# Sample-state updates cut from 128 rows to row blocks of 32, and both halves' C products added into one PSUM bank

## The chip, the cores and the metric

The kernel runs on one NeuronCore of a Trainium2 chip. The metric is device time in microseconds for one execution. The core has five engines with instruction queues of their own: TensorE (PE, matmuls and weight loads), VectorE (DVE), ScalarE (ACT), GpSimd (POOL) and SyncE (SP, which issues DMAs here). TensorE's results go to PSUM banks of 128 x 512 floats, from which VectorE and ScalarE take them.

## What is computed

One step of a hybrid decoder layer for two groups of tokens: a prompt of 272 tokens (16 meta tokens and 256) and 8 sample sequences of 4 tokens each, 304 tokens in all, 1024 channels. A SwiGLU feed-forward, a mixer, another SwiGLU, a last norm. The mixer's branch B is a state-space scan with 32 heads of 64 channels in 4 groups; B and C (128 state entries) are shared by the 8 heads of a group. The part that the change touches is the scan of the sample sequences, which bring a state of their own:

```
decay = jnp.exp(acs[:, :, -1:] - acs)
states = jnp.einsum('bcsgn,bcsgr,bcsgrp->bcgrpn', bc, decay, xdt)
chunk_decay = jnp.exp(acs[:, :, -1])
def step(h, inp):
    s, d = inp
    return h * d[..., None, None] + s, h
y_off = jnp.einsum('bcqgn,bcgrpn,bcqgr->bcqgrp', cc, h_prev, jnp.exp(acs))
```

For a sample sequence there is one chunk of 4 tokens: its new state is the old one times a decay, plus a sum over the 4 tokens of B times the decayed input; its outputs get C times the old state.

## The kernel before

**The work and its order.** `program()` writes out the order of some 1960 weight tiles of 128 x 128: first feed-forward, gates, projections into the mixer (`x`, then `ac`, `ah`, `ab`, `ya`, `z`, `gb`, `yb`, `wo`), second feed-forward. Each tile gives three one-pass matmuls (L255 to L257: high weights by high inputs, high by low, low by high), with 288 to 304 columns. I call them projections below. A unit of 8 tiles is loaded by SyncE (L174, four buffers), split into a high part by ScalarE (L183, `whi`) and a low part by VectorE (L184, `wlo`).

**The scan beside it.** The scan runs as two generators, `prompt()` and `sample()` (L904, L1039), that `drive` advances a step at a time between projections. The framework's scheduler then reorders the instructions of each engine by its own estimate, so the order of the built program isn't that of the source. Each queue runs in order. Four PSUM banks (`pss`, tag "s") are for the scan, four (`psm`, tag "m") for the projections' sums.

**The sample scan.** There are 4 groups g, and the 8 sequences come in two halves q of 4: eight units u = 2g + q. A unit's old state is a tile of 128 state entries x 4 sequences x 512 channels (`ht`, three buffers, 1 MB, loaded at L1051 and stored at L1104). For each unit:

- C by old state (L1131): four products, one for each sequence j, into partitions 32j of one bank. They are matmuls of full precision, two instructions each, 32 columns of the array by 512. ScalarE copies the bank (L1133, `yr`), four transposes turn it (L1138), VectorE multiplies by the decay (L1141).
- For each sequence, VectorE multiplies the state by its decay (L1150), TensorE makes the sum over tokens (L1152, one pass, 128 rows x 128 columns, 512 moving columns), VectorE adds it from PSUM (L1153).

The 128 rows of L1152 are the 32 sample tokens in four copies: `four` (L894) replicates the tokens, and rows 32 to 63 and 96 to 127 of the B side, and 64 to 127 of the input side, hold what rounding left over (L865, L1064), so that one pass carries all four products of high and low parts. Which sequence is meant is picked by a mask: ScalarE makes four masked copies of B for a unit (L1125, `bm`), in which 16 of the 128 rows are not zero.

`tokens(g)` (L1067) makes the inputs of a group: four transposes of the replicated sample tokens (L1078), products with dt and decay on VectorE, and the same for the prompt's last 16 tokens, whose side (`xl`, `bl`) the prompt scan uses in a matmul of 128 rows (L985), added to L984's sum. `diagonal` (L1091) makes the part within the 4 tokens, with matmuls of 48 rows and 64 columns (L1095).

`setup` (L726) runs once, some 100 us earlier: dt, its running sums by 32 small matmul instructions (L781 to L807), masks, and B's replicated side (L854 to L866).

Of the kernel before, what the change touches and what calls it, by code (L numbers as in the profile page):

```python
# [9 lines left out]
F32 = mybir.dt.float32  # L10
F32R = mybir.dt.float32r
# [6 lines left out]
P = 128  # L18
# [103 lines left out]
def tile_step(ctx: ExitStack, tc: tile.TileContext, wst: bass.AP, xT: bass.AP, vec: bass.AP,  # L122
# [469 lines left out]
    ssd = Scan(tc, mp, pss, dram, xs, V, K, h0, o_hp, o_hs)  # L592
# [113 lines left out]
class Scan:  # L706
# [3 lines left out]
    def __init__(self, tc, mp, pss, dram, xs, V, K, h0, o_hp, o_hs):  # L710
        self.nc, self.sp, self.pss, self.dram = tc.nc, mp, pss, dram
# [14 lines left out]
    def setup(self, psd, xp):  # L726
# [9 lines left out]
        act.activation(reps[:, 0].rearrange("p (k t) -> p k t", t=NL),  # L736
                       raw[:, TL:S0].unsqueeze(1).to_broadcast([P, P // NL, NL]), AF.Copy)
        act.activation(reps[:, 1].rearrange("p (k t) -> p k t", t=NB * NT),
                       raw[:, S0:T].unsqueeze(1).to_broadcast([P, 4, NB * NT]), AF.Copy)

        gtl = xp.tile([NL, P // NL, NL], F32, name="gtl")
        act.activation(gtl, K[0:NL, C_GT:C_GT + NL].unsqueeze(1).to_broadcast([NL, P // NL, NL]), AF.Copy)
# [37 lines left out]
        dl = da[0:NL, 2]  # L780
        te.matmul(pv[:, 0], lhsT=K[:, C_GT:C_GT + P], rhs=da[:, 0], start=True, stop=True)  # L781
        te.matmul(pv[:, 1], lhsT=K[:, C_GT:C_GT + P], rhs=da[:, 1], start=True, stop=False)
        te.matmul(pv[:, 1], lhsT=K[0:NL, C_ONE:C_ONE + P], rhs=dl, start=False, stop=True)
        te.matmul(pv[:, 2], lhsT=gtl.rearrange("p k t -> p (k t)"), rhs=dl, start=True, stop=True)
        te.matmul(pv[:, 3], lhsT=K[0:32, C_GTS:C_GTS + P], rhs=da[0:32, 3], start=True, stop=True)
        te.matmul(pv[:, 4], lhsT=K[:, C_ONE:C_ONE + P], rhs=da[:, 1], start=True, stop=False)
        te.matmul(pv[:, 4], lhsT=K[0:NL, C_ONE:C_ONE + P], rhs=dl, start=False, stop=True)
# [3 lines left out]
        NS = NB * NT  # L791
        NX = NS + NL


        p = self.ps()
        tri = K[:, C_TRI:C_TRI + P]
        self.cum = self.t("cum", [P, 3, H])
        te.matmul(p[:, 0:2 * H].rearrange("p (i c) -> p i c", c=H), lhsT=tri, rhs=da[:, 0:2], start=True, stop=True)
        te.matmul(p[0:32, 2 * H:3 * H], lhsT=K[0:32, C_TRIS:C_TRIS + 32], rhs=da[0:32, 3], start=True, stop=True)
        te.matmul(p[32:64, 2 * H:3 * H], lhsT=K[0:NL, C_TRI:C_TRI + 32], rhs=dl, start=True, stop=True)  # L800
        q = p[0:32, P:]
        for i in range(2):
            te.matmul(q[:, P * i:P * (i + 1)], lhsT=da[:, i], rhs=tri, start=True, stop=True)
        te.matmul(q[:, TL:S0], lhsT=da[:, 1], rhs=K[:, C_ONE:C_ONE + NL], start=True, stop=False)
        te.matmul(q[:, TL:S0], lhsT=dl, rhs=K[0:NL, C_TRI:C_TRI + NL], start=False, stop=True)
        te.matmul(q[:, S0:T], lhsT=da[0:32, 3], rhs=K[0:32, C_TRIS:C_TRIS + 32], start=True, stop=True)
        te.matmul(q[:, T:T + NL], lhsT=dl, rhs=K[0:NL, C_TRI:C_TRI + NL], start=True, stop=True)  # L807
# [22 lines left out]
        act.activation(self.mk[:, 0:P - NM], tri[:, NM:P], AF.Copy)  # L830
        act.activation(self.mk[:, P - NM:2 * P - NM], tri, AF.Copy)
        act.activation(self.mk[:, 2 * P - NM:], K[:, C_ONE:C_ONE + NL], AF.Copy)
        mks = xp.tile([NX, NX], F32, name="mks")
        pool.memset(mks, 0.0)
        act.activation(mks[0:NS, 0:NS], K[0:NS, C_TRIS:C_TRIS + NS], AF.Copy)
        act.activation(mks[NS:NX, NS:NX], K[NS:NX, C_TRI + NS:C_TRI + NX], AF.Copy)
# [17 lines left out]
        for what in ("bs", "bl"):  # L854
            rep = self.four(xp, XC, what == "bl")
            yield
            p = self.ps()
            for g in range(G):
                te.transpose(p[:, g * P:(g + 1) * P], rep[:, g], ident)
            bs = self.t(what, [P, G, P], dt=F32R)  # L860
            setattr(self, what, bs)
            pv = p.rearrange("p (g n) -> p g n", g=G)
            act.activation(bs, pv, AF.Copy)
            for a in (32, 96):
                dve.tensor_tensor(out=bs[a:a + 32], in0=pv[a:a + 32], in1=bs[a:a + 32].bitcast(F32), op=ALU.subtract)  # L865
            yield  # L866
# [5 lines left out]
    def exps(self):  # L872
# [11 lines left out]

        even = self.t("even", [P, 1])
        act.activation(even, K[:, C_BM:C_BM + 1], AF.Copy)
        for b in range(1, NL // NT):
            dve.tensor_tensor(out=even, in0=even, in1=K[:, C_BM + b:C_BM + b + 1], op=ALU.add)
        dve.tensor_scalar(out=self.dtr[:, 2], in0=self.dtr[:, 2], scalar1=even, scalar2=None, op0=ALU.mult)
# [4 lines left out]
    def four(self, pl, c0, tail=False):  # L894

        a, n = (TL, NL) if tail else (S0, NB * NT)
        self.n += 1
        r = pl.tile([P, 4, P // n, n], F32, name=f"four{self.n}", tag="tmp", bufs=2)
        src = self.xs[:, c0:c0 + 4, a:a + n].unsqueeze(2).to_broadcast([P, 4, P // n, n])
        for j in range(4):  # L900
            self.nc.scalar.activation(r[:, j], src[:, j], AF.Copy)
        return r.rearrange("p j k t -> p j (k t)")
# [136 lines left out]
    def sample(self):  # L1039
# [27 lines left out]
        def tokens(g):  # L1067
# [3 lines left out]
            for o, i in ((xst, 3), (self.xl, 2)):  # L1071
                if i == 2:
                    rep[g] = self.four(self.sp, 4 * g, True)
                    yield
# [166 lines left out]
```

## Time and profile before

| what | value |
|---|---|
| median of three runs | 881.22 us (879.95 to 882.02) |
| the profiled execution | 881.86 us |
| its span from first to last instruction | 880.0 us |
| TensorE busy | 868.8 us, 6448 matmuls |
| VectorE busy | 621.3 us |
| ScalarE busy | 496.2 us |
| mean granted TensorE clock | 0.996 |
| sample updates L1152 | 32 matmuls, 378 to 559 us into the span |
| products with C, L1131 | 64 instructions |

How to read it: a group of the profile is a line of the code with an engine, an operation, what is written and read (`out<-in`), the shape, and the number of instructions; then busy time and the mean duration in ns. PEld is TensorE's weight load, which can overlap a matmul. A shape such as 128\*32 at a matmul is the rows and columns of the array in use. A timeline row starts with the start and the duration in us. Neighbouring matmuls overlap in the records, so a matmul's price is read from the distance between starts.

### The profile page before, as it was taken

The numbers are of one execution on the slowest core, as the hardware profiler recorded it, in microseconds if no ns is written. First come the engines' busy times: TensorE is split into PE (matmuls) and PEld (weight loads), VectorE is DVE, ScalarE is ACT, GpSimd is POOL, SyncE is SP. The second block draws the span as 40 slices with busy tenths as digits, with TensorE's granted clock in tenths as the row PEclk, the third lists the DMA queues.
The fourth block names the chain that finished last, engine by engine and source line by source line (L and its number), as shares of the span: only waits on it lengthen the run. The fifth ranks groups of instructions, "written<-read, shape, count | busy, mean of one in ns | idle before, by whom it ended". The sixth has DMA issues, their size and how long they took to land.

```text
span 880.0 us, 16239 instructions
## 1 busy us (share of the span) xinstructions
PE 868.8 (99%) x6448; PEld 849.8 (97%) x6448; DVE 621.3 (71%) x996; ACT 496.2 (56%) x899; POOL 53.4 (6%) x86
## 2 busy tenths in 40 slices
PE   9999999999999999999999999999999999999996
PEld 7999999999999999999999899999999999999996
DVE  6756666554677798799988999886676666665443
ACT  8543434343667787966655687774465444444442
POOL 0000000000012233001000211100000000000000
PEclk9999999999999999999999999999999999999999
DMA  8554545454644545865666655755555555555541
GB/s 299 190 155 157 165 147 167 146 166 150 201 166 146 153 153 171 314 211 202 231 223 225 242 198 174 257 183 169 167 168 166 164 165 166 163 164 168 169 139 54
DMA packets 45851, 158.69 MB, mean 180 GB/s; under 512 B 7168, under 2 KB 9504, under 8 KB 43472
## 3 DMA queue, kind: packets, MB, share of 16 engines
q1 hardware_dynamic: 45344, 157.21, 54.6%
q8 instruction: 50, 0.82, 0.4%
q10 hardware_dynamic: 432, 0.46, 0.2%
q14 instruction: 25, 0.20, 0.1%
HBM read 145.34 MB, written 12.31 MB: 179 GB/s over the span
## 4 chain that ended last, share of the span: by engine, by line
PE 97%; DVE 1%; ACT 1%; DMA 1%; SPq 0%; issue 0%; DVEq 0%
PE ps_d L257 6%; PE ps_d L256 5%; PE ps_d L255 5%; PE ps_u L257 5%; PE ps_g L255 5%; PE ps_u L256 5%; PE ps_u L255 5%; PE ps_g L257 5%; PE ps_g L256 5%; PE ps_x L255 3%; PE ps_x L256 3%; PE ps_x L257 3%; PE ps_z L255 2%; PE ps_z L257 2%; PE ps_yb L257 2%; PE ps_yb L255 2%
## 5 line engine op out<-in xcount | busy, mean ns | idle before, releaser
L184 DVE TENSOR_TENSOR wlo<-wraw,whi 128x1024 fp32r<-128x1024 f32 (+2 forms) x250 | 300.6, 1204 | 188.8 <-ACT whi L183 188.1
L183 ACT ACTIVATE whi<-wraw 128x1024 fp32r<-128x1024 f32 (+2 forms) x250 | 259.6, 1041 | 296.8 <-issue 182.8
L257 PE MATMUL ps_d<-hh,wlo 128*128 128x304 f32 (+1 forms) x352 | 105.6, 300 | 0.0
L255 PE MATMUL ps_d<-hh,whi 128*128 128x304 f32 (+1 forms) x352 | 105.0, 299 | 0.0
L256 PE MATMUL ps_d<-hl,whi 128*128 128x304 f32 (+1 forms) x352 | 104.7, 298 | 0.0
L256 PEld LDWEIGHTS ps_d<-hl,whi 128*128 128x128 f32 x352 | 66.7, 189 | 0.0
L257 PEld LDWEIGHTS ps_d<-hh,wlo 128*128 128x128 f32 x352 | 66.2, 188 | 0.0
L255 PEld LDWEIGHTS ps_d<-hh,whi 128*128 128x128 f32 x352 | 66.1, 188 | 0.0
L255 PE MATMUL ps_x<-unh,whi 128*128 128x304 f32 x192 | 58.8, 309 | 0.7 <-ACT dtraw L735 0.7
L256 PE MATMUL ps_x<-unl,whi 128*128 128x304 f32 x192 | 58.8, 307 | 0.0
L257 PE MATMUL ps_x<-unh,wlo 128*128 128x304 f32 x192 | 58.6, 306 | 0.0
L255 PE MATMUL ps_g<-n1h,whi 128*128 128x304 f32 x176 | 54.1, 308 | 0.7 <-ACT whi L183 0.7
L256 PE MATMUL ps_u<-n1l,whi 128*128 128x304 f32 x176 | 53.6, 304 | 0.0
L255 PE MATMUL ps_u<-n1h,whi 128*128 128x304 f32 x176 | 53.5, 304 | 0.0
L256 PE MATMUL ps_g<-n1l,whi 128*128 128x304 f32 x176 | 53.4, 304 | 0.0
L257 PE MATMUL ps_g<-n1h,wlo 128*128 128x304 f32 x176 | 53.1, 303 | 0.0
L257 PE MATMUL ps_u<-n1h,wlo 128*128 128x304 f32 x176 | 52.9, 302 | 0.0
L257 PE MATMUL ps_g<-n2h,wlo 128*128 128x288 f32 x176 | 52.3, 297 | 0.0
L255 PE MATMUL ps_u<-n2h,whi 128*128 128x288 f32 x176 | 52.2, 297 | 0.0
L257 PE MATMUL ps_u<-n2h,wlo 128*128 128x288 f32 x176 | 52.1, 296 | 0.0
L255 PE MATMUL ps_g<-n2h,whi 128*128 128x288 f32 x176 | 51.9, 295 | 0.0
L256 PE MATMUL ps_u<-n2l,whi 128*128 128x288 f32 x176 | 51.4, 292 | 0.0
(342 smaller groups left out, 2435.6 us busy)
## 6 DMA issues: line engine op xcount, KB each, us to landing
wraw<-wst SPq DMA_DIRECT2D x241, 512.0 KB, 3.5
h<-h SPq DMA_DIRECT2D x8, 1024.0 KB, 5.0
o_hs<-h SPq DMA_DIRECT2D x8, 1024.0 KB, 4.3
acb<-cumd SPq DMA_DIRECT2D x8, 512.0 KB, 4.3
wraw<-wst SPq DMA_DIRECT2D x7, 256.0 KB, 6.4
hd<-h SPq DMA_DIRECT2D x1, 1216.0 KB, 6.6
h<-hd SPq DMA_DIRECT2D x1, 1216.0 KB, 8.3
o_hp<-hf SPq DMA_DIRECT2D x8, 128.0 KB, 2.8
```

The lines of the kernel that those rows point to most:

```text
L183: act.activation(hi[:, a:b], r[:, a:b], AF.Copy)
L184: dve.tensor_tensor(out=lo[:, a:b], in0=r[:, a:b], in1=hi[:, a:b].bitcast(F32), op=ALU.subtract)
L255: te.matmul(o, lhsT=wh, rhs=xh, start=first, stop=False)
L256: te.matmul(o, lhsT=wh, rhs=xl, start=False, stop=False)
L257: te.matmul(o, lhsT=wl, rhs=xh, start=False, stop=last)
```

## The change

**Rows.** The four copies of 32 tokens are laid out anew. Before, a quarter of the 128 rows was all 32 tokens in one of the four high/low combinations. After, quarter i holds two sequences only (i and 4 + i, 4 tokens each), each in all four combinations: `rows` (in the diff below) makes this layout with six ScalarE copies. So a sequence's sum needs one quarter, and the mask has to pick one of two sequences there, which is the half q: two masked copies a group in place of eight. The leftovers of rounding are made with a mask column `kd` in a `scalar_tensor_tensor` over all partitions.

**The updates.** For each half, all four decay multiplications come first, then four banks are taken (three of the scan's, one of the projections'), then four matmuls of 32 rows, one for each quarter, then four adds.

**C.** For a group, the products of both halves go into one bank: `cc` holds each sequence's 4 columns in a slot of 32 with zeros, the second half's shifted by 4, and adds to the first's. So there is one copy, one set of four transposes, and two multiplications a group. Both halves' states must be there for it.

**The prompt's last block and the small sums.** The last 16 prompt tokens now stand in rows 32 to 127 behind the 32 sample tokens (`mixed`), so that one transpose serves both (`xdts` in one operation over 48 partitions). The prompt's matmul with `bl` and `xl` uses partitions 64 to 127. In `setup` the small matmuls take 48 rows of a zero-padded tile `kx` in place of 16 or 32, and 28 instructions do the work of 32.

**Where the instructions stand now.** TensorE, in the sample scan's first group, before: `bm` is the masked B side and `xst` the inputs (the update L1152), `yr` the C product that is turned, `K` the identity, and ps_ah the projections.

```order
L257 MATMUL ps_ah_4401<-unh,wlo_4283 128x290
L1138 MATMUL sps_4296<-K,yr_4251 128x128 x4
L943 MATMUL sps_4313<-K,xs 128x128 x4
L1152 MATMUL sps_4347<-xst_4075,bm_4241 128x512
L255 MATMUL ps_ah_4401<-unh,whi_4282 128x290
```

The update stands behind two sets of transposes, ahead of projections; the next two of its unit come 46 rows further on.

TensorE in the same group now, with the prompt's state matmuls L1017 to L1019 (L983 to L985 before) and the updates L1200 of the second half, quarters 0 and 1 (up_1_0, up_1_1):

```order
L1017 MATMUL sps_4552<-xr_4348,bt_4079 128x256
L1018 MATMUL sps_4552<-xr_4348,bt_4079 128x256
L1019 MATMUL sps_4552<-xl_4157,bl_3608 128x256
L255 MATMUL ps_ac_4705<-unh,whi_4591 128x290
L256 MATMUL ps_ac_4705<-unl,whi_4591 128x290
L1200 MATMUL up_1_0_4572<-xst_4097,bm_4231 128x512
L257 MATMUL ps_ac_4705<-unh,wlo_4592 128x290
L255 MATMUL ps_ac_4705<-unh,whi_4591 128x290
L256 MATMUL ps_ac_4705<-unl,whi_4591 128x290
L257 MATMUL ps_ac_4705<-unh,wlo_4592 128x290
L1200 MATMUL up_1_1_4573<-xst_4097,bm_4231 128x512
```

The matmuls that the source writes one behind the other have projections between them; quarter 3 of this half stands 64 rows above quarter 0, and quarter 2 25 rows below quarter 1.

TensorE in the third group now, where two quarters of an update (up_0_0, up_0_1) meet:

```order
L1018 MATMUL sps_5533<-xr_5209,bt_5310 128x256
L1019 MATMUL sps_5533<-xl_5286,bl_3608 128x256
L1200 MATMUL up_0_0_5550<-xst_5245,bm_5384 128x512
L1200 MATMUL up_0_1_5551<-xst_5245,bm_5384 128x512
L257 MATMUL ps_ya_5637<-ya,wlo_5521 128x288
```

It is the one place where two of the 32 updates are neighbours.

VectorE in the first group now: the decay multiplications L1191 (L1150 before) of both halves' states h_29 and h_30, between a weight unit's low half (wlo, L184) and the next:

```order
L184 TENSOR_TENSOR wlo_4435<-wraw_4367,whi_4434 128x1024
L1127 TENSOR_TENSOR xl_4157<-xrs_4155,xl_4157 32x512
L546 TENSOR_TENSOR ya<-yat_4362,ya 128x288
L1191 TENSOR_TENSOR h_29_4042<-h_29_4042,dec_3029 128x512 x4
L1191 TENSOR_TENSOR h_30_4044<-h_30_4044,dec_3029 128x512 x4
L528 TENSOR_TENSOR ab_2513<-ps_ah_4438,act_4430 128x258
L529 TENSOR_TENSOR ab_2513<-ps_ah_4438,act_4430 128x8x4
L1202 TENSOR_TENSOR h_29_4042<-up_0_3_4418,h_29_4042 128x512
L184 TENSOR_TENSOR wlo_4485<-wraw_4432,whi_4484 128x1024
```

Eight stand in a row; before, four of one half did, with other work and the adds ahead of the next half's.

**The diff**, cut to what the text speaks of:

```diff
@@ setup @@
-        dl = da[0:NL, 2]
+        dx = da[0:NX, 2]
...
-        te.matmul(pv[:, 1], lhsT=K[0:NL, C_ONE:C_ONE + P], rhs=dl, start=False, stop=True)
-        te.matmul(pv[:, 2], lhsT=gtl.rearrange("p k t -> p (k t)"), rhs=dl, start=True, stop=True)
-        te.matmul(pv[:, 3], lhsT=K[0:32, C_GTS:C_GTS + P], rhs=da[0:32, 3], start=True, stop=True)
+        te.matmul(pv[:, 1], lhsT=one, rhs=dx, start=False, stop=True)
+        te.matmul(pv[:, 2], lhsT=gtl, rhs=dx, start=True, stop=True)
+        te.matmul(pv[:, 3], lhsT=gtr, rhs=dx, start=True, stop=True)
...
@@ the layout of rows @@
+    def mixed(self, out, x):
+        act, n = self.nc.scalar, out.shape[1]
+        k = P // NL - 2
+        act.activation(out[:, :, 0:NB * NT], x[:, :, S0:T], AF.Copy)
+        for j in range(n):
+            act.activation(out[:, j, NB * NT:].rearrange("p (k t) -> p k t", t=NL),
+                           x[:, j, TL:S0].unsqueeze(1).to_broadcast([P, k, NL]), AF.Copy)
+
+    def rows(self, pl, out, x):
+        act, (p, n, _) = self.nc.scalar, out.shape
+        self.n += 1
+        t = pl.tile([p, n, 4, 2, NT], F32, name=f"rows{self.n}", tag="rows", bufs=1)
+        for q in range(2):
+            act.activation(t[:, :, :, q], x[:, :, 16 * q:16 * q + 16].rearrange("p n (i t) -> p n i t", t=NT), AF.Copy)
+        for j in range(n):
+            act.activation(out[:, j].rearrange("p (i c w) -> p i c w", c=4, w=2 * NT),
+                           t[:, j].rearrange("p i q t -> p i (q t)").unsqueeze(2).to_broadcast([p, 4, 4, 2 * NT]),
+                           AF.Copy)
...
@@ prompt, states @@
-            te.matmul(b, lhsT=self.bl[:, g], rhs=self.xl[g][:, 2 * P * q:2 * P * (q + 1)], start=False, stop=True)
+            te.matmul(b, lhsT=self.bl[64:P, g], rhs=self.xl[g][64:P, 2 * P * q:2 * P * (q + 1)], start=False, stop=True)
...
@@ sample @@
-            bm = self.t("bm", [P, 4, P], dt=F32R)
-            for j in range(4):
-                b = C_BM + 4 * q + j
-                act.activation(bm[:, j], self.bs[:, g].bitcast(F32), AF.Copy, scale=K[:, b:b + 1])
+            bm = self.t("bm", [P, 2, P], dt=F32R)
+            for q in range(2):
+                act.activation(bm[:, q], self.bs[:, g].bitcast(F32), AF.Copy, scale=self.kd[:, 2 + q:3 + q])
...
-            for j in range(4):
-                a = 4 * NT * q + NT * j
-                te.matmul(p[32 * j:32 * j + 32], lhsT=cc[:, a:a + NS], rhs=ht[:, j], start=True, stop=True)
+            for q in range(2):
+                for j in range(4):
+                    te.matmul(p[32 * j:32 * j + 32], lhsT=cc[:, P * q + 32 * j:P * q + 32 * j + 32],
+                              rhs=hts[2 * g + q][:, j], start=q == 0, stop=q == 1)
...
-            for j in range(4):
-                o = ht[:, j]
-                oh = o.rearrange("p (h d) -> p h d", h=8)
-                dec = self.dec[:, 8 * g:8 * g + 8, 4 * q + j].unsqueeze(2).to_broadcast([P, 8, HD])
-                dve.tensor_tensor(out=oh, in0=oh, in1=dec, op=ALU.mult)
-                p = self.ps()
-                te.matmul(p, lhsT=bm[:, j], rhs=xst[g], start=True, stop=True)
-                dve.tensor_tensor(out=o, in0=p, in1=o, op=ALU.add)
+            for q in range(2):
+                ht = hts[2 * g + q]
+                for j in range(4):
+                    oh = ht[:, j].rearrange("p (h d) -> p h d", h=8)
+                    dec = self.dec[:, 8 * g:8 * g + 8, 4 * q + j].unsqueeze(2).to_broadcast([P, 8, HD])
+                    dve.tensor_tensor(out=oh, in0=oh, in1=dec, op=ALU.mult)
+                    if j % 2:
+                        yield
+                store()
+                ps = [(self.psm if j == 3 else self.pss).tile([P, 512], F32, name=f"up{g}_{q}_{j}",
+                                                             tag="m" if j == 3 else "s") for j in range(4)]
+                for j in range(4):
+                    a = slice(32 * j, 32 * j + 32)
+                    te.matmul(ps[j], lhsT=bm[a, q], rhs=xst[g][a], start=True, stop=True)
+                for j in range(4):
+                    dve.tensor_tensor(out=ht[:, j], in0=ps[j], in1=ht[:, j], op=ALU.add)
```

More of the change, by code (lines that the diff above doesn't have):

```diff
@@ L735, in setup @@
         act.activation(raw, psd, AF.Copy)
[L736 to L742, printed above, removed]
+        self.mixed(reps[:, 0:1], raw.unsqueeze(1))
+        self.rows(xp, reps[:, 1:2], raw[:, S0:T].unsqueeze(1))
+        NS = NB * NT
+        NX = NS + NL
+        tl = slice(NS, NX)
+        kx = xp.tile([NX, 3 * P + NX], F32, name="kx")
+        gtl, gtr, one, mks = (kx[:, P * i:min(P * (i + 1), 3 * P + NX)] for i in range(4))
+        pool.memset(kx, 0.0)
+        act.activation(gtl[tl].rearrange("p (k t) -> p k t", t=NL),
+                       K[tl, C_GT + NS:C_GT + NX].unsqueeze(1).to_broadcast([NL, P // NL, NL]), AF.Copy)
+        self.rows(xp, gtr[0:NS].unsqueeze(1), K[0:NS, C_GTS:C_GTS + NS].unsqueeze(1))
+        act.activation(one[tl], K[tl, C_ONE:C_ONE + P], AF.Copy)
+        act.activation(mks[0:NS, 0:NS], K[0:NS, C_TRIS:C_TRIS + NS], AF.Copy)
+        act.activation(mks[tl, tl], K[tl, C_TRI + NS:C_TRI + NX], AF.Copy)
         yield
@@ L858, in setup @@
             for g in range(G):
[L859 to L865, printed above, removed]
+                te.transpose(p[:, g * P:(g + 1) * P], r[:, g], ident)
+            o = self.t(what, [P, G, P], dt=F32R)
+            setattr(self, what, o)
+            a = slice(0 if what == "bs" else 64, P)
+            low = kd[a, 1:2] if what == "bs" else kd[a, 0:1]
+            pv = p.rearrange("p (g n) -> p g n", g=G)[a]
+            act.activation(o[a], pv, AF.Copy)
+            dve.scalar_tensor_tensor(out=o[a], in0=pv, scalar=low, in1=o[a].bitcast(F32), op0=ALU.mult,
+                                     op1=ALU.subtract)
             yield
@@ L883, in exps @@
         dve.tensor_tensor(out=self.dtr, in0=self.dt, in1=er[:, 0:4], op=ALU.mult)
[L885 to L889, printed above, removed]
+        for i in (2, 3):
+            dve.tensor_scalar(out=self.dtr[:, i], in0=self.dtr[:, i], scalar1=self.kd[:, i + 2:i + 3], scalar2=None,
+                              op0=ALU.mult)
         for g in range(G):
@@ L1067, in tokens, with turned @@
         def tokens(g):
             hs = slice(8 * g, 8 * g + 8)
[L1070 to L1074 removed]
+            def turned(src):
                 p = self.ps()
[L1076 removed]
                 for j in range(4):
                     te.transpose(p[:, j * P:(j + 1) * P], src[:, j], ident)
[L1079 to L1089 removed]
+                return p.rearrange("p (h d) -> p h d", h=8)
@@ new lines, in decayed @@
+            def decayed(pv, i, a):
+                xr = self.t("xrs", [P, 8, HD], bufs=2, tag="tmp")
+                dve.tensor_tensor(out=xr[a], in0=pv[a], op=ALU.mult,
+                                  in1=self.dtr[a, i, hs].unsqueeze(2).to_broadcast([a.stop - a.start, 8, HD]))
+                return xr.rearrange("p h d -> p (h d)")
+            xf = decayed(turned(rep.pop(g)), 3, slice(0, P))
+            o = xst[g] = self.t("xst", [P, 512], bufs=2, dt=F32R)
+            act.activation(o, xf, AF.Copy)
@@ L1091, in diagonal @@
+            while self.xl:
+                yield
+            xf = decayed(pv, 2, slice(64, P))
+            o = self.xl[g] = self.t("xl", [P, 512], dt=F32R)
+            act.activation(o[64:P], xf[64:P], AF.Copy)
+            dve.tensor_tensor(out=o[96:P], in0=xf[96:P], in1=o[96:P].bitcast(F32), op=ALU.subtract)
+            yield
         def diagonal(g):
@@ L1108, in sample @@
             load(u)
-        rep[0] = self.four(self.sp, 0)
+        cc = self.t("cc", [P, 2 * (P + NT)])
+        pool.memset(cc, 0.0)
+        rep[0] = self.sample_rows(self.sp, 0)
         yield
@@ L1168, in sample @@
+            if g + 1 < G:
+                yield from tokens(g + 1)
+                diagonal(g + 1)
+                yield
         store()
```

137 lines of the change are left out of this document (63 added, 74 removed).

## The prediction

> **What bounds the kernel now.** I read the page's busy shares and its chain first: is one engine in the way all the time, or do engines take turns?
>
> ```profile
> PE 868.8 (99%) x6448; PEld 849.8 (97%) x6448; DVE 621.3 (71%) x996; ACT 496.2 (56%) x899; POOL 53.4 (6%) x86
> PE 97%; DVE 1%; ACT 1%; DMA 1%; SPq 0%; issue 0%; DVEq 0%
> ```
>
> TensorE is busy for 99% of the span and 97% of the chain that ended last lies on it. So a nanosecond of TensorE's queue is a nanosecond of the kernel, and work on other engines is free as long as TensorE finds its operands. Next I asked for windows of the sample scan (some 360 to 560 us), where the change lies, to see how near the others are. The columns are PE, PEld, DVE, ACT and POOL busy, the granted clock, DMA share and GB/s.
>
> ```profile
> 380.00:400.00 20.00, 20.00 (x154) 18.35 (x153) 20.00 (x43) 13.45 (x29) 1.87 (x3) 1.00 0.64 222
> 460.00:480.00 20.00, 19.78 (x158) 19.09 (x157) 18.37 (x27) 12.31 (x26) 0.00 (x0) 1.00 0.60 188
> 540.00:560.00 20.00, 20.00 (x152) 18.18 (x151) 19.80 (x38) 14.61 (x25) 2.72 (x3) 1.00 0.54 191
> ```
>
> TensorE is full, but VectorE is nearly full too (20.00 of 20.00 us in one window). TensorE still sets the time, yet VectorE has no reserve here; a rival below rests on it.
>
> A busy matmul says little of what it costs, since matmuls overlap. The price is the distance between starts, so I read TensorE's timeline (start, duration, line). First a lone state update among projections, then four transposes.
>
> ```profile
> 473.40 0.29 PE L257 MATMUL ps_ya<-ya,wlo 128*128 128x288 f32 x1
> 473.54 0.29 PE L255 MATMUL ps_ya<-ya,whi 128*128 128x288 f32 x1
> 473.67 0.40 PE L1152 MATMUL sps<-xst,bm 128*128 128x512 f32 x1
> 473.90 0.30 PE L256 MATMUL ps_ya<-ya,whi 128*128 128x288 f32 x1
> ```
>
> ```profile
> 497.62 0.60 PE L943 MATMUL sps<-K,xs 128*128 128x128 f32 x4
> 497.98 0.38 PE L257 MATMUL ps_z<-unh,wlo 128*128 128x288 f32 x1
> 498.20 0.29 PE L255 MATMUL ps_z<-unh,whi 128*128 128x288 f32 x1
> ```
>
> Projections start 0.13 us apart. The update adds 473.90 - 473.67 = 0.23 us, though it shows as 0.40. From the first of four transposes to the second projection behind them is 498.20 - 497.62 = 0.58; one projection of 0.13 is in that, so four cost 0.45 us, 0.11 each. (L943 is the prompt scan's transpose; the sample's, L1138, has the same form.)
>
> **The change, part by part.**
>
> *The updates.* They stay 32 matmuls of 512 columns, with 32 rows each in place of 128.
>
> ```profile
> L1152 PE MATMUL sps<-xst,bm 128*128 128x512 f32 x32 | 13.8, 448 | 0.0
> L985 PE MATMUL sps<-xl,bl 128*128 128x256 f32 x8 | 3.1, 386 | 0.0
> ```
>
> The source writes four side by side, but the built order parts them: each stands where its PSUM bank comes free, with projections of 128 rows before and behind. I walked down TensorE's order: 32 updates make 31 runs, and one pair alone (group 2, row blocks 0 and 1) is adjacent. So there is almost nothing to overlap, and each keeps its 0.23 us. What is new is that the part of the array in use changes before and behind each. What does that cost? The nearest rows are the 48x64 matmuls among projections; first the matmuls, then the weight loads.
>
> ```profile
> 475.62 0.29 PE L257 MATMUL ps_ya<-ya,wlo 128*128 128x288 f32 x1
> 475.85 0.67 PE L1095 MATMUL sps<-ms,xdts 48*64 48x48 f32 x16
> 476.44 0.40 PE L255 MATMUL ps_ya<-ya,whi 128*128 128x288 f32 x1
> 476.68 0.29 PE L256 MATMUL ps_ya<-ya,whi 128*128 128x288 f32 x1
> ```
>
> ```profile
> 372.27 0.29 PE L257 MATMUL ps_ac<-unh,wlo 128*128 128x290 f32 x1
> ```
>
> ```profile
> 372.49 0.54 PEld L1095 LDWEIGHTS sps<-ms,xdts 48*64 48x64 f32 x16 [0.16 <-issue]
> ...
> 475.36 0.19 PEld L256 LDWEIGHTS ps_ya<-ya,whi 128*128 128x128 f32 x1
> 475.50 0.19 PEld L257 LDWEIGHTS ps_ya<-ya,wlo 128*128 128x128 f32 x1
> 475.84 0.54 PEld L1095 LDWEIGHTS sps<-ms,xdts 48*64 48x64 f32 x16 [0.16 <-DVE h L1153]
> 476.44 0.19 PEld L255 LDWEIGHTS ps_ya<-ya,whi 128*128 128x128 f32 x1
> 476.55 0.19 PEld L256 LDWEIGHTS ps_ya<-ya,whi 128*128 128x128 f32 x1
> ```
>
> Between equal shapes the next weights load while the matmul before streams: 475.36 to 475.50. At the change they do not: the load starts 0.22 us after the matmul at 475.62, that is 0.09 later than the next matmul would have started, and its own length then lies bare. That length is 476.55 - 476.44 = 0.11 for 128 columns. Together 0.20 us a change. The bracket at 475.84 names VectorE, but at 372.27 to 372.49 the same 0.22 passes with nothing waited for. Does that hold where only the rows change? The setup has such rows (16, 32 and 128 rows, always 128 columns; each line two loads):
>
> ```profile
> 278.65 0.30 PEld L782 LDWEIGHTS sps<-dta,K 128*128 128x128 f32 x2
> 278.99 0.29 PEld L783 LDWEIGHTS sps<-dta,K 16*128 16x128 f32 x2
> 279.21 0.30 PEld L784 LDWEIGHTS sps<-dta,gtl 16*128 16x128 f32 x2
> 279.43 0.30 PEld L785 LDWEIGHTS sps<-dta,K 32*128 32x128 f32 x2
> 279.77 0.30 PEld L786 LDWEIGHTS sps<-dta,K 128*128 128x128 f32 x2
> ```
>
> L783 to L784 and L784 to L785 take 0.22, so 16 and 32 rows pass as one shape. L782 to L783 (128 to 16 rows) and L785 to L786 (32 to 128) take 0.34: 0.12 more, both ways. Here loads set the pace anyway; among projections the hidden load of 0.11 is laid bare as well, which gives 0.23. My ends are 0.12 and 0.23 a change; I take 0.21, by the first row, which stands among projections.
>
> Now the count, shapes being rows (up to 32, 64 or 128) by columns. Neighbours of unlike shape: 54 in the order before, 115 after. The updates make 62 of the new ones (31 runs, in and out). The prompt's last-block matmul (L985, now L1019) drops from 128 to 64 rows behind one of 128: 8 times in and out, one of them shared with an update, so 15. The products with C come in 4 blocks in place of 8, and with their neighbours give back 16. In the setup there are 8 before and 8 after. 62 + 15 - 16 = 61, at 0.21: **+12.8 us** (7.3 to 14.0 by the ends).
>
> The Trainium skill, in "TensorE: Matmul & The Clock Gate", Part 3, has four row tiles (32 rows, 512 columns) run at once, measured 3.07 times as fast as one after another. No run here shows that, and by the order there is one pair for it.
>
> *Transposes of y.* One set of four serves both halves: 16 of 32 go, 16 x 0.11 = **-1.8 us**. C's 32 products keep their number and columns; a second accumulation into a bank adds none. The adjacent pair may save a 0.2, the setup's four matmul instructions fewer 0.1: **-0.3**.
>
> *Other engines*, at nothing beside TensorE:
>
> ```profile
> L1125 ACT ACTIVATE bm<-bs,K 128x128 fp32r<-128x128 f32 x32 | 10.2, 390 | 2.2 <-PE sps L1152 2.2
> L1082 DVE TENSOR_TENSOR xdts<-sps,dtt 16x512 f32<-16x512 f32 x4 | 2.7, 684 | 0.1
> 377.65 2.49 DVE L1150 TENSOR_TENSOR h<-h,dec 128x512 f32<-128x512 f32 x4
> h<-h SPq DMA_DIRECT2D x8, 1024.0 KB, 5.0
> o_hs<-h SPq DMA_DIRECT2D x8, 1024.0 KB, 4.3
> ```
>
> ScalarE's masks drop from 32 to 8 (-24 x 0.39 = -9.4 us), about 4 us of longer replications come back. VectorE loses one multiplication a group (-2.7 us). Both hide behind a TensorE that now has more to do. The C products wait for both halves' states: on SyncE's queue the late half's load stands behind the store of the slot's old state, 4.3 + 5.0 us, and weight loads wait behind both. From the update that frees the slot to the C product lie at least 130 projections by the order, 130 x 0.13 = 17 us. If that cover were gone, a group would lose up to 9.3 us. The bank borrowed from the projections' four costs nothing while three take turns, with 24 matmuls (3.1 us) each to be emptied.
>
> *Sum.* 12.8 - 1.8 - 0.3 = **+10.7 us**. The profiled execution took 881.86 us, so 892.6; it stood 0.64 above the median of 881.22, so I forecast **891.9 us**.
>
> **The rivals.**
>
> *VectorE makes TensorE wait.* Four decay multiplications in a row take 2.49 us; in the new order eight stand so in three of the groups (in the fourth one thing lies between), with the next weights' low halves behind them. For it: the full VectorE windows. Against it: TensorE's projections are slower to come, by 10 us over the stage. If each group loses 1 to 2.5 us beyond what is buffered, +4 to +10: 896 to 902.
>
> *The clock.* Behind the setup the granted clock fell to half:
>
> ```profile
> 278.50:282.50 4.00, 4.00 (x38) 3.67 (x37) 3.85 (x9) 2.41 (x8) 1.28 (x2) 1.00 0.54 139
> 282.50:286.00 3.50, 3.50 (x16) 3.50 (x15) 0.00 (x0) 2.15 (x5) 0.00 (x0) 0.51 0.44 155
> 286.00:294.00 8.00, 8.00 (x61) 8.00 (x60) 4.52 (x4) 4.68 (x10) 1.90 (x2) 1.00 0.70 153
> ```
>
> TensorE shows busy in all rows, but what ran before the fall were small, bare matmuls. In 3.5 us it started 16, where the pace of the last row (8.00 / 61 = 0.13) gives 27: 11 lost, 1.4 us. A dense stretch of lone updates might do the same, +1.4 each time: 893 to 895. Against it: projections stand between nearly all. The same page of the Trainium skill, in Part 1, counts idle time in a free-running window of 3.4 us; here the clock fell without any idle row.
>
> *The drop in rows is free between full-column matmuls* (the other side). If a matmul of fewer rows over all 128 columns could follow one of 128 rows without the delay, 62 + 15 changes cost nothing and the 16 given back are saved: -16 x 0.21 - 2.1 = -5.5, 875.7 us. It decides at one price: break even is where a rows-only change costs 5.5 / 77 = 0.07 us. For it: no row shows a lone 32-row matmul of this type (one pass). Against it: the 0.12 of the setup, in and out.
>
> *It does what it says.* If the chip ran the fours together, 8 blocks of about 0.25 replace 32 x 0.23 (-5.4), and changes drop by 46 to 15 (+3.2); with -1.8 and -0.1 that is -4.1: 877.1. Against it: the order, which TensorE's rows of before follow.
>
> **How the numbers follow.** Forecast 0.74 (its own range 886.4 to 893.1, the sum with 0.12 and 0.23 a change), VectorE 0.11, clock 0.05, rows free 0.04, together 0.03; 0.03 for several half-effects that meet near zero. The range takes the low end of the forecast and reaches to 897, past a clock fall or two and the near part of VectorE's case: **886.4 to 897.0**. A difference under 0.2% (1.8 us) can't be told from none with this kernel. Faster 0.07, same 0.03, slower 0.90.
>
> **What would show it.** Right: the new update L1200 stands alone on the timeline, and from the projection before it to the one behind are about 0.78 us (0.36 + 2 x 0.21), where a lone L1152 took 0.36; its weights' load starts 0.2 us after that projection; L1019 likewise; the transposes L1176 count 16; TensorE's wait list stays near empty. Wrong in size: the same, with another step than 0.2. Wrong altogether: lone updates at 0.36, or several of the four starting within nanoseconds of one another; or long waits of the L255 to L257 rows on wlo (VectorE's rival), or a second stretch at a clock of 0.5.

## The result and the profile after

The changed kernel takes 891.47 us (median of 4 runs, 890.69 to 892.56), the kernel before 881.62 us in runs beside it (4 runs, 879.95 to 882.50). The ratio is 1.0115, 95% interval 1.0096 to 1.0134: slower by about 9.9 us. The forecast was 891.9. The profiled execution of after took 891.47 us, with a span of 889.7; that of before 881.86, so the two profiles differ by 9.6.

First the same two lines of the page as before, busy time of each engine and the chain that ended last:

```profile
PE 877.2 (99%) x6428; PEld 846.3 (95%) x6428; DVE 619.8 (70%) x1002; ACT 490.2 (55%) x892; POOL 58.9 (7%) x87
PE 98%; DMA 1%; ACT 1%; DVE 0%; SPq 0%; issue 0%; DVEq 0%
```

TensorE executes 20 matmul instructions fewer and is busy 8.4 us longer. VectorE and ScalarE are no busier than before; GpSimd is, by 5.5 us. Is TensorE waiting for someone? Its whole list of waits in after (what it worked on, whom it waited for, us, times, longest):

```profile
PE ps_g L255 <- ACT whi L183: 1.7, 2, 1.5
PE warm_ps L422 <- POOL warm L419: 1.3, 1, 1.3
PE ps_x L255 <- ACT dtraw L735: 0.7, 1, 0.7
PE nf_ss L280 <- ACT nf_sq L335: 0.3, 1, 0.3
```

These are 4.0 us, none of them at an update, and before's list had 3.2. So the loss lies inside TensorE's own queue. There stands the new update, L1200, alone among projections; the timeline of one such update and its neighbours (start, duration):

```profile
434.72 0.30 PE L255 MATMUL ps_ah<-unh,whi 128*128 128x290 f32 x1
434.85 0.30 PE L256 MATMUL ps_ah<-unl,whi 128*128 128x290 f32 x1
434.99 0.30 PE L257 MATMUL ps_ah<-unh,wlo 128*128 128x290 f32 x1
435.21 0.50 PE L1200 MATMUL up<-xst,bm 32*128 32x512 f32 x1
435.64 0.40 PE L255 MATMUL ps_ah<-unh,whi 128*128 128x290 f32 x1
435.88 0.29 PE L256 MATMUL ps_ah<-unl,whi 128*128 128x290 f32 x1
```

and of the weight loads in the same stretch:

```profile
434.72 0.19 PEld L256 LDWEIGHTS ps_ah<-unl,whi 128*128 128x128 f32 x1
434.86 0.19 PEld L257 LDWEIGHTS ps_ah<-unh,wlo 128*128 128x128 f32 x1
435.21 0.18 PEld L1200 LDWEIGHTS up<-xst,bm 32*128 32x128 f32 x1 [0.17 <-issue]
435.64 0.19 PEld L255 LDWEIGHTS ps_ah<-unh,whi 128*128 128x128 f32 x1 [0.25 <-issue]
435.75 0.19 PEld L256 LDWEIGHTS ps_ah<-unl,whi 128*128 128x128 f32 x1
```

Between projections the next weights load while the matmul before still streams (434.72, 434.86). At the update they do not: its load and its matmul both stand at 435.21, 0.22 us after the projection at 434.99, and the next projection's load only at 435.64. From 434.99 to 435.88 there are 0.89 us for two projections (0.27, as from 434.72 to 434.99) and the update, so the update costs 0.89 - 0.27 = 0.62 us. A lone L1152 in before cost 0.23. Two changes of shape cost 0.62 - 0.23 = 0.39, **0.195 us each**. This place is no exception: 23 of the updates in after have two projections on each side, and they cost 0.61 to 0.63 us by the same reckoning; the 14 such updates in before cost 0.22 to 0.23.

The starts also show where the 0.39 lies. The update starts 0.22 behind the projection, 0.09 more than the usual 0.13; the next projection starts 0.43 behind the update, 0.20 more than 0.23; and the one after that 0.24 further on, 0.11 more than 0.13. Read as a delay of 0.09 and a bare load of 0.11 at each of the two changes, they add up to 0.40.

The one pair that the order left adjacent shows what the edit was written for:

```profile
479.62 0.38 PE L1019 MATMUL sps<-xl,bl 64*128 64x256 f32 x1
479.94 0.50 PE L1200 MATMUL up<-xst,bm 32*128 32x512 f32 x2
480.37 0.53 PE L257 MATMUL ps_ya<-ya,wlo 128*128 128x288 f32 x2
```

Two matmuls (x2) together show 0.50 us, the duration of one, and the next projection starts 0.43 us later, as behind the lone one (435.21 to 435.64). In the records their starts are 479.939 and 479.942. So two row tiles (matmuls on different blocks of rows) do run at once on the chip, where they are neighbours.

### The profile page after: what moved, and what is told of

Its sections match the earlier page's. It is cut to its first block, busy times and chain, and to the rows that moved or that the text cites. A ratio compares the mean times of both kernels' runs of the same rounds, so it can differ in the third digit from the quotient of the medians.

```text
span 889.7 us, 16204 instructions
## 1 busy us (share of the span) xinstructions
PE 877.2 (99%) x6428; PEld 846.3 (95%) x6428; DVE 619.8 (70%) x1002; ACT 490.2 (55%) x892; POOL 58.9 (7%) x87
## 4 chain that ended last, share of the span: by engine, by line
PE 98%; DMA 1%; ACT 1%; DVE 0%; SPq 0%; issue 0%; DVEq 0%
PE ps_d L257 5%; PE ps_d L256 5%; PE ps_d L255 5%; PE ps_u L257 5%; PE ps_g L255 5%; PE ps_u L256 5%; PE ps_u L255 5%; PE ps_g L257 5%; PE ps_g L256 5%; PE ps_x L255 3%; PE ps_x L256 3%; PE ps_x L257 3%; PE ps_z L256 2%; PE ps_z L255 2%; PE ps_z L257 2%; PE ps_yb L257 2%
## 5 line engine op out<-in xcount | busy, mean ns | idle before, releaser
L184 DVE TENSOR_TENSOR wlo<-wraw,whi 128x1024 fp32r<-128x1024 f32 (+2 forms) x250 | 300.8, 1205 | 191.7 <-ACT whi L183 191.2
```

Source lines behind the costliest of these rows:

```text
L184: dve.tensor_tensor(out=lo[:, a:b], in0=r[:, a:b], in1=hi[:, a:b].bitcast(F32), op=ALU.subtract)
```

## The experiments

Theory A: each change of array shape between neighbours on TensorE costs about 0.195 us, and the order has 65 of them more. Rivals: R1, row tiles run one after the other even when adjacent; R2, the loss comes from something else in the change (the fourth bank, the half-wise states); R3, the price grows with the rows left idle. In the first expectations R2 is called theory B and R1 theory C. The diffs are cut to the lines that carry the edit; their old side is the changed kernel, and added lines shift the line numbers of later rows by a few.

**All rows in one matmul (update_128_rows).**

```
-                    a = slice(32 * j, 32 * j + 32)
-                    te.matmul(ps[j], lhsT=bm[a, q], rhs=xst[g][a], start=True, stop=True)
+                    te.matmul(ps[j], lhsT=bm[:, q], rhs=xst[g], start=True, stop=True)
```

> The changed kernel, with each update matmul taken over all 128 rows (its mask then lets the half's four sequences through, so a sequence's new state gets all four sums: the sums of the states differ from the reference). Everything else, the merged products with C and the bursts on VectorE among it, stays. Shape changes: 47 in place of 106. Theory A: 59 x 0.195 = 11.5 us less, 880.0 us, about the kernel before, a little under it. Theory B (the loss is the bursts on VectorE or the order): stays at 889 to 892.

Measured 880.49 us, ratio to before 0.9992 (0.9982 to 1.0001). The same place on the timeline:

```profile
430.19 0.30 PE L257 MATMUL ps_ah<-unh,wlo 128*128 128x290 f32 x1
430.32 0.40 PE L1199 MATMUL up<-xst,bm 128*128 128x512 f32 x1
430.56 0.30 PE L255 MATMUL ps_ah<-unh,whi 128*128 128x290 f32 x1
430.69 0.30 PE L256 MATMUL ps_ah<-unl,whi 128*128 128x290 f32 x1
```

From 430.19 to 430.69 is 0.50, less two projections: 0.23. Everything else of the change (the fourth bank, states by halves, C into one bank, 16 transposes fewer) is still in this kernel, and the loss is gone. R2 falls.

**Half the rows (update_64_rows).**

```
-                    a = slice(32 * j, 32 * j + 32)
+                    a = slice(64 * (j // 2), 64 * (j // 2) + 64)
```

> The changed kernel with each update over 64 rows instead of 32 (two sequences' sum in each state, so that part of the computation is changed); the order has 105 changes of shape, as many as the changed kernel's 106. Theory A (a change costs the same whatever the two shapes): 891.3 us. Rival R3 (the price grows with the rows left idle, so that 64 rows cost about two thirds of 32): 887 us.

Measured 892.81 us, ratio 1.0124 (1.0107 to 1.0141). A lone update in it:

```profile
436.29 0.29 PE L257 MATMUL ps_ah<-unh,wlo 128*128 128x290 f32 x1
436.51 0.49 PE L1200 MATMUL up<-xst,bm 64*128 64x512 f32 x1
436.94 0.40 PE L255 MATMUL ps_ah<-unh,whi 128*128 128x290 f32 x1
437.17 0.30 PE L256 MATMUL ps_ah<-unl,whi 128*128 128x290 f32 x1
```

The spacing is that of 32 rows (0.88 against 0.89). The price is for changing the shape, not for the rows left idle: R3 falls. The time is 1.5 us above the 891.3 expected; the profiled execution had 3.4 us at half clock behind the setup, and after's had none (below).

**The prompt's correction over 128 rows (prompt_128_rows).** Its B side gets zeros in rows 0 to 63.

```
-            te.matmul(b, lhsT=self.bl[64:P, g], rhs=self.xl[g][64:P, 2 * P * q:2 * P * (q + 1)], start=False, stop=True)
+            te.matmul(b, lhsT=self.bl[:, g], rhs=self.xl[g][:, 2 * P * q:2 * P * (q + 1)], start=False, stop=True)
```

> The changed kernel, with the prompt's last-block matmul back on 128 rows (the added 64 rows are zeros on one side, so its result stays). Shape changes: 91 in place of 106. Theory A: 15 x 0.195 = 2.9 us less, 888.6 us. If only the 32-row updates cost, or only lone matmuls among projections do: 891.5.

Measured 889.66 us, 1.8 below the changed kernel; 2.9 were expected. The same stretch in after, and in this kernel (L1018 is L1021 there, L1019 L1022, L977 L980):

```profile
432.51 0.59 PE L1018 MATMUL sps<-xr,bt 128*128 128x256 f32 x2
433.04 0.38 PE L1019 MATMUL sps<-xl,bl 64*128 64x256 f32 x1
433.35 0.66 PE L977 MATMUL sps<-K,xs 128*128 128x128 f32 x4
433.93 0.49 PE L1200 MATMUL up<-xst,bm 32*128 32x512 f32 x1
```

```profile
432.90 0.60 PE L1021 MATMUL sps<-xr,bt 128*128 128x256 f32 x2
433.14 0.47 PE L1022 MATMUL sps<-xl,bl 128*128 128x256 f32 x1
433.45 0.60 PE L980 MATMUL sps<-K,xs 128*128 128x128 f32 x4
433.98 0.50 PE L1203 MATMUL up<-xst,bm 32*128 32x512 f32 x1
```

From the first L1018 to the update 1.42 us pass in after, 1.08 here: the pair of changes costs 0.34, or 0.17 each, a little less than at the updates; why is not shown. Eight pairs make 2.7. The clock accounts for the rest: this execution had a half-clock stretch behind the setup, the profiled execution of after had none (below).

**Four in a row by force (four_together, together_and_prompt_128).** A critical section around the four matmuls; in the second kernel with the edit of prompt_128_rows as well.

```
-                for j in range(4):
+                with self.tc.tile_critical():
+                    for j in range(4):
```

> The changed kernel, with the four update matmuls of a half bound together, so that in TensorE's order nothing stands between them (8 runs of four in place of 31 runs). Shape changes between neighbours on TensorE, counted from the built orders without the setup: 106 in the changed kernel, 64 here. Theory A (each change of the array's rows or columns costs about 0.2 us, and row blocks that are neighbours run at the same time, as the one adjacent pair in the changed kernel did, 2 ns apart): 42 x 0.195 = 8.2 us less, and 8 x 0.23 in place of 31 x 0.23 us of streaming, 5.3 less: 891.5 - 13.5 = 878 us, under the kernel before (881.6). Theory B (the loss is VectorE's burst of decay multiplications, or other waits): unchanged, 889 to 892, or worse since four banks must be free at once. Theory C (changes cost, but the four stream one after another): 883.

> Both: the four update matmuls bound together and the prompt's last-block matmul on 128 rows. Shape changes: 48 in place of 106. Theory A: 58 x 0.195 + 5.3 = 16.6 us less, 875 us, faster than both kernels. Theory B: 889 to 892.

Measured 911.96 us (ratio 1.0350, 1.0330 to 1.0369) and 908.26 us (1.0307, 1.0288 to 1.0326), where 878 and 875 were expected: both misses. The longest waits of TensorE in four_together:

```profile
PE up L1202 <- DMA wraw<-wst: 4.1, 1, 4.1
PE sps L1044 <- DVE yo L1182: 3.2, 1, 3.2
PE ps_ya L255 <- PEq L1199: 3.2, 1, 3.2
PE up L1202 <- DMA o_hp<-hf: 2.7, 1, 2.7
```

one of the fours, and a window behind such a wait (the seventh entry is the granted clock):

```profile
438.58 0.51 PE L1202 MATMUL up<-xst,bm 32*128 32x512 f32 x4 [1.03 <-ACT whi L183]
```

```profile
381.50:391.50 10.00, 6.12 (x32) 4.90 (x33) 7.95 (x20) 4.37 (x12) 0.00 (x0) 0.50 0.18 65
```

At the section's edges TensorE waits for things that are no operands of the four (a weight load from memory, a store); the 3.2 us at L1044 are the wait that claimed_fours shows below. The list adds up to 26.5 us against 3.2, and the clock stood at 0.50 for 30.7 us in all, which costs half of that. 912.69 (its profiled time) - 23.3 - 15.4 = 874.0. So this pair doesn't test the theory by its total; but four matmuls in 0.51 us speak against R1.

**Four in a row by claims (claimed_fours, claimed_128_rows).** VectorE writes one number into each of the four banks, the first matmul's last, so that none can start until all four banks are free; an order without waits is kept among the four. In claimed_128_rows each then runs over all rows.

```
+                behind = mybir.DependencyInfo(mybir.DependencyClass.NoSync, mybir.DependencyReason.DATA)
+                last = None
+                for j in (1, 2, 3, 0):
+                    c = dve.memset(ps[j][0:1, 0:1], 0.0)
+                    if last is not None:
+                        self.tc.add_manual_dep(c.ins, last, behind, reason="claims in order")
+                    last = c.ins.name
```

> The changed kernel, but VectorE writes one number into each of an update's four banks before the first matmul (the first matmul's bank last), and the four matmuls stand in a row on TensorE: the order then has all 32 updates in eight runs of four, with no critical section. Theory A (each change of array shape between neighbours costs about 0.195 us, and four neighbours on different row tiles run at once): changes fall from 106 to 63, 43 x 0.195 = 8.4 us, and three of four matmuls of 0.22 us are hidden in each of eight fours, 5.3 us; 891.5 - 13.7 = 877.8 us if the 32 small writes hold nobody up, with an L1209 group that shows starts within nanoseconds of each other. If TensorE has to wait for the claims, up to 8 us more, seen as idle time before L1209 with DVE as its releaser. Rival R1 (neighbours on different row tiles run one after the other): 883. Rival R2 (the loss has nothing to do with the shape changes, but with the fourth bank or the half-wise states): 891.

> As claimed_fours, but each of the four matmuls runs over all 128 rows (the states then sum over all four sequences of the half, so that part of the computation is changed). It shows what the claims and the runs of four cost without row tiles. Theory A: changes as before's, 48 instead of 106, no hidden streaming; if the claims are free, the time of update_128_rows, 880.5 us, 2.4 above claimed_fours (15 changes fewer, 2.9 us, but 5.3 of streaming more). If the claims make TensorE wait, this kernel shows the wait alone as its distance from 880.5. R2: 891.

Measured 885.77 us (1.0055, 1.0042 to 1.0067) and 889.57 us (1.0092, 1.0079 to 1.0106). One four in claimed_fours, then the same four in claimed_128_rows:

```profile
389.05 0.30 PE L255 MATMUL ps_ah<-unh,whi 128*128 128x290 f32 x1
389.28 0.51 PE L1209 MATMUL up<-xst,bm 32*128 32x512 f32 x4
389.71 0.41 PE L256 MATMUL ps_ah<-unl,whi 128*128 128x290 f32 x1
389.96 0.29 PE L257 MATMUL ps_ah<-unh,wlo 128*128 128x290 f32 x1
```

```profile
389.14 0.29 PE L255 MATMUL ps_ah<-unh,whi 128*128 128x290 f32 x1
389.27 1.09 PE L1209 MATMUL up<-xst,bm 128*128 128x512 f32 x4
390.20 0.29 PE L256 MATMUL ps_ah<-unl,whi 128*128 128x290 f32 x1
390.33 0.30 PE L257 MATMUL ps_ah<-unh,wlo 128*128 128x290 f32 x1
```

Four row tiles cost 389.96 - 389.05 - 0.27 = 0.64 us, as much as one alone in after (0.62). Four matmuls of 128 rows cost 390.33 - 389.14 - 0.27 = 0.92. R1 falls: side by side works and is worth 0.28 us a four, 2.2 us over eight fours; the two kernels differ by 3.8 where 2.4 was expected, in the same direction (their profiled executions by 2.5). But both stand 8 to 9 us above what was expected of them without waits, and claimed_128_rows 9.1 above update_128_rows, so that is the price of the claims and of the order that comes with them. Where it lies, in claimed_fours, by its longest wait and the window behind it:

```profile
PE sps L1044 <- DVE yo L1182: 3.3, 1, 3.3
```

```profile
381.20:388.00 6.80, 5.24 (x30) 4.89 (x31) 6.07 (x20) 3.23 (x10) 0.00 (x0) 0.50 0.06 19
```

The list of waits adds up to 8.4 us, 5.2 more than before's, and 6.8 us at clock 0.50 cost 3.4. What does VectorE do before `yo`?

```profile
377.44 4.90 DVE L1192 TENSOR_TENSOR h<-h,dec 128x512 f32<-128x512 f32 x8
382.27 0.35 DVE L1182 TENSOR_TENSOR yo<-sps,ec 128x64 f32<-128x64 f32 x2
```

It works through the eight decay multiplications of the change, and `yo` stands behind them. They stand in a row in the changed kernel too (4.90 us from 377.08), but there 24 projections stand between the C products L1168 and the transposes behind them. With the claims none does, and the scan's small steps follow one another to L1044, which needs a bank that VectorE has not read yet. The prediction's VectorE rival had these eight in a row hold up the next weights' low halves; here they hold up `yo`, and only where the cover is gone. The claims are not late themselves (no update stands in the list of waits); the order that they bring about has taken the cover away.

**Claims moved or given to another engine.** claimed_fours_prompt_128 has the prompt's edit too; in claims_from_second and claims_from_second_prompt_128 the first four go without claims; in claims_by_scalar_prompt_128 ScalarE writes them.

```
-                for j in (1, 2, 3, 0):
+                for j in (1, 2, 3, 0) if g + q else ():
```

```
-                    c = dve.memset(ps[j][0:1, 0:1], 0.0)
+                    c = act.activation(ps[j][0:1, 0:1], K[0:1, 0:1], AF.Copy)
```

> As claimed_fours, and the prompt's correction matmul (64 rows before) made over 128 rows, with zeros in the upper 64. Theory A: 48 changes of shape instead of 106, 58 x 0.195 = 11.3 us, and 5.3 us of hidden streaming: 891.5 - 16.6 = 874.9 us, below the kernel before by 6.5 us. R1: 880. R2: 891.

> As claimed_fours, but the first half of the first quarter is updated as in the changed kernel, without claims; in claimed_fours TensorE's waits (5.5 us, of which 3.3 for yo) and the half clock behind them (6.83 us, 3.4 us lost) stood there. 64 changes of shape in the order against the changed kernel's 106. Theory A: 42 x 0.195 = 8.2 us and about 5.0 us of hidden streaming off 891.5, so 878.3 us, if no wait comes at the next four; seven us or so more if it does (rival R4: the claims make TensorE wait wherever they first stand), 885.

> As claims_from_second, with the prompt's correction matmul over 128 rows: 48 changes against 106. Theory A: 58 x 0.195 = 11.3 us and 5.0 us off 891.5, so 875.2 us, or claimed_fours_prompt_128 (883.8) less its 5.3 us of waits and 3.4 us of clock, 875.1; faster than the kernel before by 6 us. R4: 882 to 884, slower than before.

> As claimed_fours_prompt_128, but ScalarE writes the claims instead of VectorE; 48 changes against 106. Theory A: the waits before the first four were for VectorE's yo, moved behind other work by the order that the claims made; if ScalarE's claims leave that order as it was, 875 us; if not, 880 to 884, with the releaser named in TensorE's list of waits. R2 (shape changes don't matter): 891.

Measured, in this order: 883.81 us (1.0033, 1.0021 to 1.0046), 884.35 (1.0035, 1.0023 to 1.0047), 880.76 (0.9998, 0.9987 to 1.0010; 12 runs from 878.45 to 883.34) and 884.61 (1.0040, 1.0027 to 1.0054). Theory A had expected 874.9, 878.3, 875.2 and 875, and missed all four. For ScalarE's claims 880 to 884 had been named if the order moved as with VectorE's; that is what came, 0.6 above it (`yo` was waited for again, 3.1 us). Without claims at the first four the wait for yo is gone, but one came where the next updates stand, in claims_from_second_prompt_128:

```profile
PE up L1212 <- DVE xs L1056: 1.9, 1, 1.9
```

R4 had said 885 for claims_from_second, which came within 0.7, and 882 to 884 for claims_from_second_prompt_128, which lies between R4 and theory A. The best of the four can't be told from the kernel before and takes 10.7 us less than the changed one.

**The other part alone (c_merged_full_rows).** Updates over all rows as in before, with B zero outside a sequence's rows; C merged as in the change; the prompt's edit.

```
+                    if j % 2 == 0:
+                        bm = self.t("bm", [P, 2, P], dt=F32R)
+                        for i in range(2):
+                            b = 4 * q + j + i
+                            act.activation(bm[:, i], self.bs[:, g].bitcast(F32), AF.Copy, scale=kq[:, b:b + 1])
+                    te.matmul(ps[j], lhsT=bm[:, j % 2], rhs=xst[g], start=True, stop=True)
```

> The changed kernel with one part of its change undone: each update runs over all 128 rows again, with a B that is zero outside its own sequence's rows (24 more copies on ScalarE, as before), in two pairs of each half; C times both halves' states still goes into one bank (16 transposes fewer than the kernel before), and the prompt's correction matmul is made over 128 rows with zeros. No claims. The order has 32 changes of shape, against 106 in the changed kernel and 41 in the kernel before. Theory A: 74 x 0.195 = 14.4 us off 891.5, 877.1 us; or from the kernel before: 881.4 - 9 x 0.195 - 16 x 0.11 = 877.9; 877.5 us, faster than both, with no update above 0.23 us. Rival R2 (the loss lies in the half-wise states and the fourth bank, not in the shapes): 889 to 891. Rival R5 (the 24 copies and B's small buffer make TensorE wait for ScalarE): 880 to 885, with bm among TensorE's releasers.

Measured 892.37 us (1.0135, 1.0113 to 1.0158), a miss of 15 us that lies above R5's 880 to 885 too, and next to R2's 889 to 891. But R2 has no place for what the trace shows: R5's waits for `bm`, a longer wait beside them, and the clock behind it:

```profile
PE sps L1046 <- DVE yo L1186: 4.8, 1, 4.8
PE up L1209 <- ACT bm L1208: 3.9, 2, 2.2
```

```profile
383.00:396.60 13.60, 9.06 (x38) 7.48 (x39) 11.63 (x27) 6.37 (x18) 0.00 (x0) 0.50 0.27 103
```

A lone update costs 0.23 us here, as expected (436.20 to 436.43). The waits for `bm` alone, 3.9 us, are more than the 9 changes of shape saved against before (1.8). The wait for `yo` stands behind eight decay multiplications again (4.90 us from 380.13); which part of the edit moved it there isn't shown. What the merged C alone would bring with a B buffer of the old size was not tried.

**All of them in one table.** "Changes" are changes of shape in each kernel's order, without the setup's. From each profiled time I take TensorE's waits above before's 3.2 us, and half of the time that the clock stood at half speed before TensorE's last matmul. This is rough: where a wait lies in a half-clock stretch, part of it is taken off twice.

| kernel | changes | profiled us | waits | at half clock | less both |
|---|---|---|---|---|---|
| before | 41 | 881.86 | 3.2 | 3.4 | 880.2 |
| after | 106 | 891.47 | 4.0 | 0 | 890.7 |
| update_64_rows | 105 | 892.76 | 3.6 | 3.4 | 890.7 |
| prompt_128_rows | 91 | 889.98 | 3.2 | 3.4 | 888.3 |
| update_128_rows | 47 | 879.72 | 2.6 | 0 | 880.3 |
| claimed_128_rows | 48 | 889.81 | 8.8 | 10.2 | 879.1 |
| claimed_fours | 63 | 887.28 | 8.4 | 10.2 | 877.0 |
| claims_from_second | 64 | 882.98 | 5.5 | 3.4 | 879.0 |
| claimed_fours_prompt_128 | 48 | 883.81 | 8.1 | 6.8 | 875.5 |
| claims_from_second_prompt_128 | 48 | 880.38 | 5.9 | 3.4 | 876.0 |
| claims_by_scalar_prompt_128 | 48 | 884.23 | 9.7 | 6.8 | 874.3 |
| c_merged_full_rows | 32 | 895.45 | 14.2 | 20.5 | 874.2 |
| four_together | 64 | 912.69 | 26.5 | 30.7 | 874.0 |
| together_and_prompt_128 | 48 | 910.75 | 28.3 | 27.3 | 872.0 |

In the first five rows, where little is taken off, the last column follows the count: the two kernels with 105 and 106 changes agree, and 15 changes fewer give 2.4 us less. Of the two kernels with the same claims, claimed_fours stands 2.1 us below claimed_128_rows though it has 15 changes more. Where more is taken off, the column is too low: four_together and claims_from_second both have 64 changes of shape and stand 5 us apart. So the last rows show no more than that waits and clock are large enough to account for those misses.

## Why the prediction was right, point by point

- **A shape change costs 0.21 us**: 0.195 at the updates, 0.17 at L1019. The reading from the 48x64 rows, a delay of 0.09 and a bare load of 0.11, held for a change of rows alone. The setup's 0.12 with a bare load of 0.11 beside it, 0.23, was too much. The sign named for a lone update, 0.78 us from the projection before to the one behind, came as 0.65 (434.99 to 435.64): 0.11 of the second change falls behind that projection.
- **61 changes more, from 54 to 115**: miscounted. A recount of the orders gives 49 and 114 with the setup's 8, so 65 more; the C products gave back 12, not 16. By the measured prices the term is 50 x 0.195 + 15 x 0.17 = 12.3 us, against 12.8. That the term came out so close is luck: the count was 4 too low and the price too high, and the two errors nearly cancel.
- **Transposes -1.8 and small savings -0.3**: L1176 counts 16; the sum of both was not measured by itself, and update_128_rows, which keeps both and has 6 changes more than before, stands at 880.3 against 880.2 in the last column, where -2.1 + 6 x 0.195 = -0.9 was due, a difference of 1.0 us. Half of it lies behind TensorE's last matmul (8.6 us to the end of the span, 8.1 in before); the rest stays unexplained.

The clock was not in the sum, and moved the result of one execution. Before's profile lost 11 starts behind the setup; after's did not, in the same window:

```profile
282.50:286.00 3.50, 3.50 (x26) 3.50 (x27) 0.28 (x2) 3.18 (x7) 0.00 (x0) 1.00 0.51 164
```

26 matmuls start in a window in which before started 16: 10 x 0.13 = 1.3 us given back, in this execution. prompt_128_rows, with the same setup, fell to 0.50 there again; update_128_rows did not. The executions of before alone show mean clocks from 0.994 to 0.998, where a stretch of 3.4 us at half clock makes 0.002. So I take it to change from one execution to the next, and not for an effect of the change.

- **Other engines at nothing; VectorE makes TensorE wait**: it did not in this kernel. Waits grew by 0.8 us, and at whi some 10 us into the span, not at wlo. In claimed_fours, four_together and c_merged_full_rows the eight multiplications in a row did make TensorE wait, 3.2 to 4.8 us.
- The balance of the two profiles: 12.3 - 2.1 - 1.3 + 0.8 = 9.7, and 0.5 behind TensorE's last matmul as above, 10.2; measured 9.6.
- **It does what it says**: right about the chip, wrong about the order. Its 877.1 us is where claimed_fours stands without its waits and clock (877.0), but that is in part chance: the rival counted 15 changes more than before, claimed_fours has 22, and the correction is rough.
- **Rows free**: fell, with 0.62 us for a lone update.

The Trainium skill, in "TensorE: Matmul & The Clock Gate", Part 3, says that row tiles run concurrently with starts a few nanoseconds apart. The traces agree: in claimed_fours a four starts at 431.765, 431.769, 431.772 and 431.775. In "TensorEngine Tiling (Array Packing)", Key Properties, the same skill says that changing the tiling mode drains the engine. The traces fit this as far as they go: at a change the next weights do not load while the matmul before streams. They give the price that decided this case, 0.195 us each way.

## What to carry to other kernels

Row tiles pay only as neighbours: count the changes of array shape in the built order, at what one costs in your trace, before you count what overlaps. Here a lone 32-row matmul among 128-row ones cost 0.62 us against 0.23, and four together 0.64 against 0.92, so the whole gain of eight perfect fours (2.2 us) was a fifth of the loss from 65 changes (12.3). When you bind instructions together to save such a cost, look at TensorE's list of waits again: each binding here moved other work and cost 2 to 25 us in waits, and all but one of them time at half clock in or behind the waits. Then look at what stands ahead of the awaited result on its own engine: in claimed_fours it was eight multiplications, which had cost nothing as long as projections covered them.

## What the runs showed of the hardware

- Four matmuls of 32 rows on different row blocks start within 10 ns and end together; the four cost what one costs.
- The price of a shape change was the same to and from 32 and 64 rows (0.62 us for a lone update in both), and the same for 23 lone updates of 32 rows (0.61 to 0.63).
- Half-clock stretches came in pieces of 3.41 us and multiples (3.4, 6.8, 10.2 and 13.7 in a row). The Trainium skill, in "TensorE: Matmul & The Clock Gate", Part 1, has a free-running window of 3413 ns, which fits these lengths, and says that an idle window brings the slow clock. During the wait of 3.3 us in claimed_fours, which ended at 382.8, the clock fell, at 381.2. But the length of a wait alone does not decide it: 2.0 us in claims_from_second was followed by a stretch from 392.6 to 396.0, and 1.9 us in c_merged_full_rows (to 10.5) by one from 10.9 to 14.3, while 1.9 us in claims_from_second_prompt_128 and 2.2 us in c_merged_full_rows (to 541.9) were not. Behind the setup it came and went with no wait at all. What besides idle time decides it stays open.
